# One series of scores for the first two token tiles of a differential head, a price for changes of rows in the planner, and the first norm's sums on VectorE

## The chip, the cores and the metric

The kernel runs on one core of a Trainium2 chip. The metric is the device time of one execution in microseconds (us), the median of several runs. Engines: PE is the matmul engine (PEld its weight loads), DVE is VectorE, ACT is ScalarE, POOL is GpSimd, SP issues the DMAs.

## The reference

A trunk of two residual layers on 512 tokens of 1024 features, in float32. Layer 0 mixes tokens with retention, layer 1 with differential attention in six heads; each layer also attends to 256 memory tokens and ends with a SwiGLU feed-forward part. What the change touches:

```python
def rms_norm(x, w):
    y = x32 * lax.rsqrt(jnp.mean(x32 * x32, axis=-1, keepdims=True) + EPS)
...
    h = rms_norm(x, attn_norm_w[layer])
    u = h @ w_in[layer]
...
        sc = jnp.einsum('bihcd,bjhcd->bhcij', qblk, k).astype(jnp.float32) * scale
        dist = jnp.abs(t[:, None] - s_pos[None, :]).astype(jnp.float32)
        bias = -slopes[:, None, None] * dist[None]
        allowed = s_chunk[None, :] <= (t // CHUNK)[:, None]
        sc = jnp.where(allowed, sc + bias[None, :, None], -jnp.inf)
        p = jax.nn.softmax(sc, axis=-1)
        a = p[:, :, 0] - lam * p[:, :, 1]
        return jnp.einsum('bhij,bjhe->bihe', a.astype(v.dtype), v)
```

A differential head has two score maps, each from 64 features, whose softmaxes are subtracted. Queries go in blocks of 128 tokens and see the keys up to their own chunk.

## The kernel before, in words

**Layout and precision.** x stands transposed in eight tiles `xT` of 128 features x 512 tokens. A float32 product is made of three matmuls of a faster type: each operand is split into a high half (`wh` of weights, made by ACT) and a low half (`wl`, the rest, made by DVE, or POOL in some chunks of layer 1), and `mm3` adds high by high, high by low and low by high. Weights come by DMA in chunks into three pages `wr`, and each chunk is split once, for three pages of either half.

**The planner.** The program is written out by Python, with one stream of main matmuls and many generators for side work (norms, softmaxes, transposes, splits). `Weave` keeps a clock for each engine. Each operation passes through `Engine.go` (lines 263 to 291), which counts a cost for it (`us`): a matmul of 128 rows with n columns n / 2400 + 0.0134; one with 64 rows 0.11 + 0.00012 n; a DVE operation 0.07 + 0.00104 n; a POOL addition 0.17 + 0.0021 n. It then moves that engine's clock, waiting for what the operands need. After each matmul of the main stream `pump` lets those side generators go on whose due time has come on PE's clock. So these costs set the order in which each engine's instructions stand; on the chip every engine takes them in that order. Pages and banks are counted in `free`; `take` waits until there are enough, `give` returns them.

**The first token norm.** For each feature tile `NormX.tile` (line 613) multiplies by the norm's weight, splits (ACT then DVE), waits (in the first norm alone 4.0 us, `later`), squares on ACT into a `tab` page of which there are three, and adds the square to the first tile's, on POOL (line 630). After the eighth, `token_norm` (line 544) sums over features with four small matmuls against ones, and the power -0.5 follows on POOL. Meanwhile the main stream runs the first projection (`tok_block`, `first=True`): chunk by chunk, 24 matmuls each, as tiles and chunks arrive. Splits of chunk 3 are queued on ACT and DVE when the stream comes to chunk 2.

**The differential heads.** `lane` (line 1248) starts the units of the two heads of a projected pair: for each head `unit` once for each of four token tiles a, as soon as the tile's queries and keys are ready and the unit before has sent its exponentials. `unit` (line 1132) makes the two score maps in two banks with `mm3_pair`: six matmuls of 64 rows and (a + 1) * 128 columns, in three pairs, the first map on partitions 0 to 63 and the second on 64 to 127. DVE adds the position bias and takes the minimum (the scores are negated); ACT exponentiates with the row sum; DVE forms the quotient `rho` and the difference of the maps. Every second unit transposes the differences of two tiles and multiplies by the values.

**The second norm's halves.** `token_halves` (line 1343) makes differences and sums of token halves for a fast matrix product, in `wk` pages.

Of the kernel before, what the change touches and what calls it, by code (L numbers as in the profile page):

```python
# [14 lines left out]
AF = mybir.ActivationFunctionType  # L15
# [3 lines left out]
P = 128  # L19
# [137 lines left out]
class Weave:  # L157
# [7 lines left out]
    def __init__(self):  # L165
        self.n, self.q = 0, []
        self.clock = {"pe": 0.0, "dve": 0.0, "act": 0.0, "pool": 0.0, "dma": 0.0}
        self.written = {}
        self.slots, self.slot, self.seen = {}, {}, {}
        self.port = {"dve": [], "pool": []}  # L170
        self.last = self.cur = self.now = 0.0
# [82 lines left out]
class Engine:  # L254
# [5 lines left out]
    def __getattr__(self, op):  # L260
        call = getattr(self.engine, op)

        def go(out, *args, **kw):
# [4 lines left out]
            if self.name == "pe":  # L268
                us = max(0.108, n / 2400 * (1 if op == "transpose" or kw["rhs"].dtype == F32R else 4) + 0.0134)
                if ins[0].shape[0] == 64:  # L270
                    us = 0.11 + 0.00012 * n
            elif self.name == "act":
                us = 0.09 + 0.00084 * n + 0.19 * ("accum_out" in kw) + 0.05 * isinstance(kw.get("scale"), bass.AP)
            elif self.name == "pool":
                us = 0.3 + 0.165 * n if kw.get("op") == ALU.pow else 0.17 + 0.0021 * n
            elif self.name == "dma":
                us = n * P * 4 / 360e3
            else:
                us = 0.07 + 0.00104 * n + 0.06 * any(free_size(v) == 1 and n > 1 for v in ins[1:])
# [13 lines left out]
def body(ctx: ExitStack, tc: tile.TileContext, x_d, mem_d, w_d, par_d, dec_d, ali_d, out_d):  # L293
# [309 lines left out]
    class NormX:  # L603
# [9 lines left out]
        def tile(self, k):  # L613
# [14 lines left out]
            else:  # L628
                yield
                G.tensor_tensor(self.sq_sum, self.sq_sum, sq, op=ALU.add)  # L630
# [453 lines left out]
    def diff_layer(layer, xw, nrm, mem_norm):  # L1084
# [47 lines left out]
        def unit(h, a, qT, kT, st):  # L1132
            n = (a + 1) * P
            u = a // 2
            ts = slice(a * P, (a + 1) * P)
            es = slice(h * P, (h + 1) * P)
            pages = st["pages"][u]
            if u == 0:
                pr = [pages[c][:, a * P:a * P + n] for c in range(2)]
            else:  # L1140
                pr = [pages[2 * (a - 2) + c][:, :n] for c in range(2)]
            st["p"][a] = pr[0]
            mn, s1, rho = small(2), small(2), small(1)
# [10 lines left out]
            for c in range(2):  # L1154

                V.tensor_tensor_reduce(pr[c], scs[c][:, :n], st["ali"][:, T - n:], scale=1.0, scalar=3.0e38,
                                       op0=ALU.add, op1=ALU.min, accum_out=mn[:, c:c + 1])
                ends.append(W.last + 0.13)
# [3 lines left out]
            for c in range(2):  # L1162
                W.cur = ends[c]
                yield
                dst = st["s0"][:, a:a + 1] if c == 0 else s1[:, 0:1]
                A.activation(pr[c], pr[c], AF.Exp, bias=mn[:, c:c + 1], scale=-1.0, accum_out=dst)
# [81 lines left out]
        def lane(p, res, ready):  # L1248
# [9 lines left out]
            for i in range(2):  # L1258
                st = {"ali": alis[i], "s0": page("s0", [P, TT], 6), "av": 0, "started": 0, "p": {}, "done": set(),
                      "pages": [[], []]}  # L1260
                for a in range(TT):
                    pages = 2 * (a // 2) + 2 if a % 2 == 0 else 0
                    while free["wk"] < pages or st["started"] < a or a not in ready or W.backlog() > BACKLOG:
                        yield 0.3
                    yield from take(wk=pages)
                    st["pages"][a // 2] += [wk([P, T]) for _ in range(pages)]
                    W.add(unit(2 * p + i, a, res[i], res[2 + i], st))
# [75 lines left out]
    def token_halves(layer, norm, tb):  # L1343
# [7 lines left out]
        def sums(j):  # L1351
# [5 lines left out]
            z = [wk([P, T])[:, s] for _ in range(3) for s in (a, b)]  # L1357
# [375 lines left out]
```

## Time and profile before

| what | us |
| --- | --- |
| median of 3 runs | 1141.38 |
| lowest and highest of them | 1139.38, 1141.46 |
| the profiled execution | 1143.51 |
| its span, first to last instruction | 1141.7 |
| mean granted clock of PE over the span | 0.997 of full |

Every instruction goes through line 287, so groups of the profile are told apart by engine, operation and tile names: `out<-in`, then the shape, then the count (x6). Two rows with one name in the timeline are merged where nothing else of that engine stands between. Times are from the span's start.

### The profile page before, as it was taken

What the parts mean: (1) busy time and instruction counts of PE and PEld (TensorE: products, weight loads), DVE (VectorE), ACT (ScalarE), POOL (GpSimd) and SP (SyncE); (2) the same over time, 40 slices, a digit from 0 to 9 for tenths busy, and PEclk for the clock granted to TensorE, in tenths of its full rate; (3) what the DMA queues carried; (4) which work ended last, traced back from release to release, by engine and by line L of the source; (5) the groups of instructions that cost most, each with busy time, mean ns of one, the idle gap of its engine ahead of it and who ended that gap; (6) DMA issues with size and microseconds to landing.
All of it is one profiled execution on the core that took longest, in us unless ns stands there. A gap on an engine that the chain in (4) does not pass through costs nothing.

```text
span 1141.7 us, 18447 instructions
## 1 busy us (share of the span) xinstructions
PE 1130.7 (99%) x6917; PEld 999.2 (88%) x6917; DVE 892.6 (78%) x1717; ACT 626.8 (55%) x1291; POOL 157.8 (14%) x105
## 2 busy tenths in 40 slices
PE   9999999999999999999999999999999999999998
PEld 7788888889999999998888877888899999999987
DVE  5669895799997878887657577967989987788862
ACT  6557773545564445555466575745556554455540
POOL 4120010400000000000362653343000000000000
PEclk9999999999999999999999999999999999999999
DMA  6341222332342333334231311122332333223332
GB/s 212 126 143 61 74 74 75 111 93 92 118 136 84 103 110 102 97 112 159 68 116 58 111 61 51 57 74 93 94 108 89 125 105 123 86 93 102 96 111 76
DMA packets 46600, 113.54 MB, mean 99 GB/s; under 512 B 5296, under 2 KB 17968, under 8 KB 46512
## 3 DMA queue, kind: packets, MB, share of 16 engines
q1 hardware_dynamic: 46368, 112.35, 30.5%
q8 instruction: 54, 0.88, 0.3%
q14 instruction: 34, 0.28, 0.1%
q10 hardware_dynamic: 144, 0.03, 0.0%
HBM read 110.26 MB, written 2.10 MB: 98 GB/s over the span
## 4 chain that ended last, share of the span: by engine, by line
PE 91%; DVE 3%; ACT 3%; POOL 1%; issue 1%; DMA 1%; SPq 0%; DVEq 0%; ACTq 0%
PE ps L287 91%; DVE wk L287 1%; POOL tab L287 1%; ACT wk L287 1%; DVE sm L287 1%; DMA wr<-w_t 1%; ACT wh L287 0%; DVE qk L287 0%; ACT qk L287 0%; ACT mkY L287 0%; DVE mkL L287 0%; SPq L287 0%; ACT L287 0%; ACT qc L287 0%; ACT xw L287 0%
## 5 line engine op out<-in xcount | busy, mean ns | idle before, releaser
L287 PE MATMUL ps<-xw,wh 128*128 128x256 f32 (+1 forms) x1032 | 211.6, 326 | 0.0
L287 ACT ACTIVATE wk<-ps 128x256 f32<-128x256 f32 (+3 forms) x214 | 90.8, 427 | 168.2 <-PE ps L287 167.2
L287 PE MATMUL ps<-xw,wl 128*128 128x256 f32 (+1 forms) x948 | 179.0, 306 | 0.0
L287 PEld LDWEIGHTS ps<-xw,wh 128*128 128x128 f32 x1032 | 154.4, 190 | 15.5
L287 PE MATMUL ps<-wh,xw 128*128 128x512 f32 (+1 forms) x512 | 151.1, 375 | 1.0 <-DVE qk L287 1.0
L287 PEld LDWEIGHTS ps<-xw,wl 128*128 128x128 f32 x948 | 131.2, 190 | 7.4
L287 PE MATMUL ps<-qk,wl 128*128 128x512 f32 (+1 forms) x528 | 135.6, 386 | 0.0
L287 ACT ACTIVATE wh<-wr 128x512 fp32r<-128x512 f32 (+1 forms) x144 | 118.6, 827 | 27.2 <-PE ps L287 20.9
L287 DVE TENSOR_TENSOR wl<-wk,wl 128x512 fp32r<-128x512 f32 (+3 forms) x150 | 94.4, 630 | 29.0 <-ACT wl L287 28.2
L287 PEld LDWEIGHTS ps<-qk,wl 128*128 128x128 f32 x528 | 96.1, 188 | 18.3
L287 ACT ACTIVATE wl<-wk 128x512 fp32r<-128x512 f32 (+3 forms) x150 | 85.6, 571 | 40.1 <-DVE wk L287 25.7
L287 PEld LDWEIGHTS ps<-wh,xw 128*128 128x128 f32 x512 | 92.8, 191 | 16.5 <-DVE qk L287 1.5
L287 POOL TENSOR_TENSOR tab<-tab,tab 128x512 f32<-128x512 f32 x31 | 47.2, 1524 | 431.9 <-DVE v L287 306.7
L287 PE MATMUL ps<-v,wh 128*128 128x256 f32 x792 | 106.1, 279 | 0.0
L287 PE MATMUL ps<-qk,wh 128*128 128x512 f32 (+1 forms) x393 | 104.4, 387 | 0.5 <-DVE qk L287 0.5
L287 DVE TENSOR_TENSOR wh<-wk,wh 128x512 fp32r<-128x512 f32 (+3 forms) x130 | 79.2, 609 | 26.7 <-ACT wh L287 26.7
L287 PEld LDWEIGHTS ps<-v,wh 128*128 128x128 f32 x792 | 98.3, 189 | 0.0
L287 PE MATMUL ps<-wl,xw 128*128 128x512 f32 (+1 forms) x256 | 96.0, 375 | 0.9 <-DVE wl L287 0.9
L287 ACT ACTIVATE wh<-wk 128x512 fp32r<-128x512 f32 (+3 forms) x130 | 72.6, 559 | 42.5 <-DVE wk L287 34.6
L287 DVE TENSOR_TENSOR xT<-ps,xT 128x512 f32<-128x512 f32 (+1 forms) x81 | 55.1, 680 | 50.9 <-PE ps L287 50.6
L287 PEld LDWEIGHTS ps<-qk,wh 128*128 128x128 f32 x393 | 71.9, 188 | 15.6 <-DVE qk L287 1.1
L287 PE MATMUL ps<-v,wl 128*128 128x256 f32 x576 | 77.4, 279 | 0.0
(169 smaller groups left out, 1969.7 us busy)
## 6 DMA issues: line engine op xcount, KB each, us to landing
wr<-w_t SPq DMA_DIRECT2D x148, 512.0 KB, 3.5
wk<-w_t SPq DMA_DIRECT2D x48, 192.0 KB, 3.8
wk<-w_t SPq DMA_DIRECT2D x32, 256.0 KB, 3.9
wk<-w_t SPq DMA_DIRECT2D x32, 128.0 KB, 3.4
wr<-w_t SPq DMA_DIRECT2D x8, 256.0 KB, 5.2
xT<-x_t SPq DMA_DIRECT2D x8, 256.0 KB, 5.5
zo<-mem_t SPq DMA_DIRECT2D x8, 256.0 KB, 6.0
out_t<-xT SPq DMA_DIRECT2D x7, 256.0 KB, 2.0
```

The source lines that it names most:

```text
L287: return call(out, *args, **kw)
```

## The change

Four things. (1) `Engine.go` adds 0.19 to a matmul whose rows differ from those of the matmul before it. (2) The sums of the squares of the norm with `later` (the first) go to DVE. (3) `unit` takes a group of token tiles: (0, 1) in one unit, then 2, then 3. The group's scores lie side by side in the same two banks and are made in one run of twelve matmuls; the minimum passes, exponentials, one reciprocal and one `rho` for the group follow. A group starts when its last tile is ready. (4) `token_halves` takes three `wk` pages and cuts each in two halves, where it called for six pages.

```diff
+        self.rows = 128
...
                 if ins[0].shape[0] == 64:
                     us = 0.11 + 0.00012 * n
+
+                us += 0.19 * (ins[0].shape[0] != self.weave.rows)
+                self.weave.rows = ins[0].shape[0]
...
-                G.tensor_tensor(self.sq_sum, self.sq_sum, sq, op=ALU.add)
+                (V if self.later else G).tensor_tensor(self.sq_sum, self.sq_sum, sq, op=ALU.add)
...
-        def unit(h, a, qT, kT, st):
-            n = (a + 1) * P
+        def unit(h, group, qT, kT, st):
+            a, g = group[-1], len(group)
...
+            cols = {b: slice(b * P, b * P + (b + 1) * P) if u == 0 else slice(0, (b + 1) * P) for b in group}
+            pr = {b: [pages[c if u == 0 else 2 * (b - 2) + c][:, cols[b]] for c in range(2)] for b in group}
+            mn, s1, rho = small(2 * g), small(2 * g), small(g)
             yield from take(ps=2)
-            scs, pair = [bank(), bank()], []
-            for c in range(2):
-                rows = slice(c * DH, (c + 1) * DH)
-                pair.append((scs[c][:, :n], [z[rows, ts] for z in qT], [z[rows, :n] for z in kT]))
-            mm3_pair(pair)
+            scs = [bank(), bank()]
+            for b in group:
+                st["p"][b] = pr[b][0]
+                ts, keys, pair = slice(b * P, (b + 1) * P), slice(0, (b + 1) * P), []
+                for c in range(2):
+                    rows = slice(c * DH, (c + 1) * DH)
+                    pair.append((scs[c][:, cols[b]], [z[rows, ts] for z in qT], [z[rows, keys] for z in kT]))
+                mm3_pair(pair)
...
-            V.reciprocal(s1[:, 1:2], s1[:, 0:1])
-            V.scalar_tensor_tensor(rho, st["s0"][:, a:a + 1], lam, s1[:, 1:2], op0=ALU.mult, op1=ALU.mult)
+            V.reciprocal(s1[:, g:2 * g], s1[:, :g])
+            V.scalar_tensor_tensor(rho, st["s0"][:, group[0]:a + 1], lam, s1[:, g:2 * g], op0=ALU.mult, op1=ALU.mult)
 
-            V.scalar_tensor_tensor(pr[0], pr[1], rho, pr[0], op0=ALU.mult, op1=ALU.add)
-            st["done"].add(a)
+            for i, b in enumerate(group):
+                V.scalar_tensor_tensor(pr[b][0], pr[b][1], rho[:, i:i + 1], pr[b][0], op0=ALU.mult, op1=ALU.add)
+            st["done"].update(group)
...
-                for a in range(TT):
-                    pages = 2 * (a // 2) + 2 if a % 2 == 0 else 0
-                    while free["wk"] < pages or st["started"] < a or a not in ready or W.backlog() > BACKLOG:
+                for group in ((0, 1), (2,), (3,)):
+                    a = group[-1]
+                    pages = (2, 4, 0)[a - 1]
+                    while free["wk"] < pages or st["started"] < group[0] or a not in ready or W.backlog() > BACKLOG:
...
-            z = [wk([P, T])[:, s] for _ in range(3) for s in (a, b)]
+            z = [w[:, s] for w in [wk([P, T]) for _ in range(3)] for s in (a, b)]
```

## Rows read from the trace of the kernel before

**Rows 1.** The page, part 1: busy us (share of the span) and instructions by engine.

```profile
PE 1130.7 (99%) x6917; PEld 999.2 (88%) x6917; DVE 892.6 (78%) x1717; ACT 626.8 (55%) x1291; POOL 157.8 (14%) x105
```

**Rows 2.** Windows: stretch, us, busy of PE, PEld, DVE, ACT, POOL, PE's clock, DMA, GB/s.

```profile
650.00:675.00 25.00, 24.65 (x143) 18.26 (x142) 16.38 (x62) 14.13 (x39) 9.71 (x6) 1.00 0.30 97
675.00:700.00 25.00, 23.78 (x140) 18.55 (x139) 20.14 (x60) 16.57 (x47) 11.16 (x8) 1.00 0.21 69
800.00:825.00 25.00, 25.00 (x115) 20.77 (x114) 24.71 (x56) 14.59 (x28) 1.02 (x1) 1.00 0.33 98
```

**Rows 3.** Timeline of PE, 23 to 34: start, us, what, [idle before <-releaser].

```profile
23.21 0.74 PE L287 MATMUL ps<-wh,xw 128*128 128x512 f32 x2
24.52 0.50 PE L287 MATMUL ps<-wl,xw 128*128 128x512 f32 x1 [0.57 <-DVE wl L287]
25.66 1.52 PE L287 MATMUL ps<-ones,tab 128*128 128x1 f32 x8 [0.63 <-POOL tab L287]
27.03 1.20 PE L287 MATMUL ps<-wh,xw 128*128 128x512 f32 x2
28.03 0.63 PE L287 MATMUL ps<-wl,xw 128*128 128x512 f32 x1
28.46 1.05 PE L287 MATMUL ps<-wh,xw 128*128 128x512 f32 x2
...
33.04 0.39 PE L287 MATMUL ps<-wl,xw 128*128 128x512 f32 x1
```

**Rows 4.** A window of 1 us there: columns as in rows 2.

```profile
31.00:32.00 1.00, 1.00 (x4) 0.79 (x3) 0.75 (x2) 0.24 (x2) 0.68 (x1) 0.50 0.70 244
```

**Rows 5.** Timelines of POOL, ACT and DVE, 14 to 28.

```profile
14.88 10.72 POOL L287 TENSOR_TENSOR tab<-tab,tab 128x512 f32<-128x512 f32 x7 [13.57 <-ACT tab L287]
...
20.88 0.63 ACT L287 ACTIVATE tab<-xT 128x512 f32<-128x512 f32 x1 [0.74 <-POOL tab L287]
...
22.79 2.51 ACT L287 ACTIVATE wh<-wr 128x512 fp32r<-128x512 f32 x3
...
14.50 0.75 DVE L287 SCALAR_TENSOR_TENSOR xw<-xT,par,xw 128x512 fp32r<-128x512 f32 x1
15.96 0.99 DVE L287 SCALAR_TENSOR_TENSOR xw<-xT,par,xw 128x512 fp32r<-128x512 f32 x1 [0.72 <-ACT xw L287]
22.07 0.70 DVE L287 TENSOR_TENSOR wl<-wr,wh 128x512 fp32r<-128x512 f32 x1 [5.11 <-ACT wh L287]
23.43 4.38 DVE L287 TENSOR_TENSOR wl<-wr,wh 128x512 fp32r<-128x512 f32 x3 [0.67 <-ACT wh L287]
```

**Rows 6.** Timeline of PE around two series of 64 rows, 652 to 657.

```profile
652.91 0.62 PE L287 MATMUL ps<-wh,xw 128*128 128x512 f32 x2
653.47 0.55 PE L287 MATMUL ps<-qk,qk 64*128 64x128 f32 x6
653.95 0.50 PE L287 MATMUL ps<-wl,xw 128*128 128x512 f32 x1
654.28 0.63 PE L287 MATMUL ps<-wh,xw 128*128 128x512 f32 x2
654.75 0.40 PE L287 MATMUL ps<-wl,xw 128*128 128x512 f32 x1
655.07 0.62 PE L287 MATMUL ps<-qk,qk 64*128 64x256 f32 x6
655.62 0.74 PE L287 MATMUL ps<-wh,xw 128*128 128x512 f32 x2
656.21 0.40 PE L287 MATMUL ps<-wl,xw 128*128 128x512 f32 x1
```

**Rows 7.** Timelines of PE and DVE: a wait, and two small operations of a unit.

```profile
685.00 0.50 PE L287 MATMUL ps<-wh,xw 128*128 128x512 f32 x1 [1.02 <-DVE qk L287]
...
673.16 0.15 DVE L287 RECIPROCAL sm<-sm 128x1 f32<-128x1 f32 x1
673.35 0.22 DVE L287 SCALAR_TENSOR_TENSOR sm<-s,der,sm 128x1 f32<-128x1 f32 x1
```

More of the change, by code (lines that the diff above doesn't have):

```diff
@@ L1130, in qk_proj @@
             W.add(lane(p, res, ready))
-        def unit(h, a, qT, kT, st):
-            n = (a + 1) * P
+        def unit(h, group, qT, kT, st):
+            a, g = group[-1], len(group)
             u = a // 2
-            ts = slice(a * P, (a + 1) * P)
             es = slice(h * P, (h + 1) * P)
             pages = st["pages"][u]
[L1138 to L1143, printed above, removed]
-            yield from take(ps=2)
-            scs, pair = [bank(), bank()], []
-            for c in range(2):
-                rows = slice(c * DH, (c + 1) * DH)
-                pair.append((scs[c][:, :n], [z[rows, ts] for z in qT], [z[rows, :n] for z in kT]))
-            mm3_pair(pair)
+            cols = {b: slice(b * P, b * P + (b + 1) * P) if u == 0 else slice(0, (b + 1) * P) for b in group}
+            pr = {b: [pages[c if u == 0 else 2 * (b - 2) + c][:, cols[b]] for c in range(2)] for b in group}
+            mn, s1, rho = small(2 * g), small(2 * g), small(g)
+            yield from take(ps=2)
+            scs = [bank(), bank()]
[6 more added lines that the diff above has]
+                mm3_pair(pair)
             if a == TT - 1:
@@ L1153, in unit @@
             ends = []
[L1154 to L1158, printed above, removed]
+            for i, b in enumerate(group):
+                for c in range(2):
+                    V.tensor_tensor_reduce(pr[b][c], scs[c][:, cols[b]], st["ali"][:, T - (b + 1) * P:], scale=1.0, scalar=3.0e38,
+                                           op0=ALU.add, op1=ALU.min, accum_out=mn[:, 2 * i + c:2 * i + c + 1])
+                    ends.append(W.last + 0.13)
             give("ps", 2)
@@ L1161, in unit @@
                 give("tab", 1)
[L1162 to L1166, printed above, removed]
+            for i, b in enumerate(group):
+                for c in range(2):
+                    W.cur = ends[2 * i + c]
+                    yield
+                    dst = st["s0"][:, b:b + 1] if c == 0 else s1[:, i:i + 1]
+                    A.activation(pr[b][c], pr[b][c], AF.Exp, bias=mn[:, 2 * i + c:2 * i + c + 1], scale=-1.0, accum_out=dst)
             st["started"] = a + 1
             yield
-            V.reciprocal(s1[:, 1:2], s1[:, 0:1])
-            V.scalar_tensor_tensor(rho, st["s0"][:, a:a + 1], lam, s1[:, 1:2], op0=ALU.mult, op1=ALU.mult)
-            V.scalar_tensor_tensor(pr[0], pr[1], rho, pr[0], op0=ALU.mult, op1=ALU.add)
-            st["done"].add(a)
+            V.reciprocal(s1[:, g:2 * g], s1[:, :g])
+            V.scalar_tensor_tensor(rho, st["s0"][:, group[0]:a + 1], lam, s1[:, g:2 * g], op0=ALU.mult, op1=ALU.mult)
+            for i, b in enumerate(group):
+                V.scalar_tensor_tensor(pr[b][0], pr[b][1], rho[:, i:i + 1], pr[b][0], op0=ALU.mult, op1=ALU.add)
+            st["done"].update(group)
             if a % 2 == 0:
@@ L1266, in lane @@
                     st["pages"][a // 2] += [wk([P, T]) for _ in range(pages)]
-                    W.add(unit(2 * p + i, a, res[i], res[2 + i], st))
+                    W.add(unit(2 * p + i, group, res[i], res[2 + i], st))
                     yield 0.5
```

## The prediction

> **What bounds the kernel now.** I read the page first, then the windows of 25 us, then PE's timeline where a window looked odd. The page has PE busy for 99% of the span [rows 1], so a saving counts only if it takes work or waiting off PE itself, and a cost only if PE waits for it. That busy share hides something: PE's record of a matmul runs on while it waits inside the pipeline, and what tells of lost time is the weight loads, of which each matmul has one. In an ordinary stretch, 800 to 825, they are busy for 20.8 of 25 us; in 650 to 675, with PE still at 24.65, only for 18.3 [rows 2]. From there on I measure lost time by the starts of successive matmuls. A full 128x512 matmul takes 0.23 us from start to start (two from 654.28 to 654.75 [rows 6]). Two places of the change lose time by that measure.
>
> *The start.* From 23.21 to 33.04 us PE needs 9.83 us for 17 matmuls of 512 columns (2, 1, 2 and 12 in rows that alternate) and the eight small ones of the first token norm [rows 3]. At full pace these are 17 x 0.23 = 3.9, and about 0.9 for the eight (they took 1.37, most of it at half clock, so between 0.7 and 1.4). So 5.0 us are lost: first a wait for a weight split (0.57 idle, DVE wl), then one for the last sum (0.63 idle, POOL tab), and behind the two the granted clock falls to 0.5, from 2.4 to 1.2 GHz, until about 33 us: 128x512 matmuls have a spacing of 0.43 (28.03 to 28.46), and the window at 31 shows the clock [rows 3, 4]. Both waits go back to POOL. Its seven sums run from 14.88 for 10.72 us, 1.53 each. ACT's squares wait for the pages that they free (0.74 idle before the one at 20.88), the weight split's ACT half stands behind those squares and starts at 22.79, and DVE, after 5.11 us without work, gets its half late and then takes 4.38 us for three splits, of which the first kind alone takes 0.70: it runs slowly beside POOL [rows 5].
>
> *The score series.* A series of six 64-row matmuls costs PE, for 128 columns, 654.28 - 652.91 = 1.37 less three ordinary ones, 0.68 us; for 256 columns 656.21 - 654.75 = 1.46 less three, 0.77 us [rows 6]. The six run as three pairs side by side. Three pairs at half of 0.23 would be 0.35 for 256 columns, which leaves 0.42; for 128 columns the pairs can't cost more than that, which leaves at least 0.33. So 0.33 to 0.42 of each series is a fixed price of entering and leaving it, seen as late starts on both sides: 653.47 where the row before would end its turn at 653.37, and 0.33 instead of 0.23 behind 653.95.
>
> **The change, part by part.** The sum is made against the profiled execution, 1143.51 us (span 1141.7 and 1.8 around it), which lies 2.1 over the median of 1141.38; differences are carried to the median.
>
> *Sums on VectorE.* Seven POOL additions go, seven DVE additions come, at 0.65 to 0.70 each by the 128x512 TENSOR_TENSOR at 22.07 [rows 5]: 4.9 us of DVE work into a stretch where it idles 5.11 and 0.72. Squares still need the three tab pages, each freed by the sum before last. DVE is done with the seventh tile's split at 14.50 + 0.75 = 15.25. From there seven sums and the last token tile's split (0.75) run back to back to 20.9, or to 21.6 if the first weight split of chunk 3 gets in ahead of the last sum. The order of PE is set by the planner: with 0.60 in place of 1.245 for a sum, and the last square still held 4 us behind its split, I count the norm's matmuls some 15 places into chunk 2, whose first matmul stands at 17.3 (chunk 3's is two matmuls ahead of the row at 23.21, at 22.8, and 24 at the planner's 0.227 come before it). PE comes there at 17.3 + 15 x 0.227 = 20.7. An estimate from both: a wait of 0.2 to 0.9, and I take 0.9. Queued on DVE behind sums that wait for squares are the splits of chunk 3, which PE wants at 22.8 and which, sent straight after, are ready by about 22: no second wait. One pause of 0.9 is shorter than the two together, and around the idle 1.02 at 685.00 [rows 7] the granted clock stayed at 1.00 [rows 2], so I take it to stay up. Gain 5.0 - 0.9 = 4.1; between 0 (the pause and the fall stay) and 5.0 (no pause).
>
> *One series for token tiles 0 and 1.* Six heads lose one entry and exit each. No row has a series that changes its width inside. The bounds are 0 (the width costs what the row change costs) and 0.42; the nearest row is the series itself, whose pairs change their weights twice without a late start of that size, so I take 0.36: 6 x 0.36 = 2.2 us.
> The Trainium skill (TensorEngine Tiling (Array Packing), section Key Properties) says that changing the tiling mode, not just the tile, drains the engine. By that a change of width inside the series drains nothing and the 2.2 stand, where the lower bound above would make them 0; no run here has shown such a series yet.
>
> *DVE beside it.* One reciprocal (0.15) and one small product (0.22) [rows 7] go per head, 2.2 us in all, under PE's matmuls and worth nothing where they are covered. At 685.00, where PE idles 1.02 for DVE, they may take up to 0.4 off; I count 0.2. The four minimum passes now stand in one block on DVE and hold two banks until the last of them, 0.4 to 0.8 us longer; what waits behind it is the next projection's norm, and that is how the wait at 685.00 came about, so this may also give those 0.2 back. The first pair of scores also waits for the second token tile, 6 x 0.23 = 1.4 us later; the lane has the next projection's matmuls as cover, and without it PE would wait those 1.4 once.
>
> *The estimate.* Before, the planner took 6 x (0.11 + 0.00012 x 128) = 0.75 for a series that measures 0.68, and 0.84 for 0.77: right within 0.07. It now adds 0.19 for each change of rows to a price that already held it. A series at 384 or 512 columns is over by 0.38; the joined one is put at 0.75 + 0.84 + 0.38 = 1.97 against 0.68 + 0.77 - 0.36 = 1.09, over by 0.88. Over six heads that is 6 x (0.88 + 0.38 + 0.38) = 9.8 us by which PE arrives before the planner expects it, at transposes and products whose input another engine is still making. Cover: the exit's part is right for work that starts from that series (its end and the next matmul's delay are now put where the trace has them), and waits that the planner itself foresees on PE are swallowed first. I take a sixth, 1.6 us of new waits, between 0 and 9.8.
>
> *Page reuse in the second norm's halves.* Three wk pages per pair in place of six names for them; the instructions are the same. At 800 to 825, with DVE at 24.7 of 25, PE was full [rows 2]: nothing. If that cover went, a late split of 0.7 per pair would show.
>
> Sum: -4.1 - 2.2 - 0.2 + 0.2 + 1.6 = -4.7: 1138.8 for this execution, 1136.7 against the median.
>
> **The rivals.**
> - *The pause keeps its price* (chance 0.12). The sums on DVE still end after PE arrives, PE pauses as long as before and the clock falls. For it: the planner moves PE's place forward by nearly as much as the sum. Against it: 5.11 us of DVE idle and no POOL beside it. The start then gains nothing: 1136.7 + 4.1 = 1140.8, no change to be told.
> - *The padded estimate becomes waits* (0.08). At the transposes and value products of layer 1, 650 to 760 us, PE stands for what it is ahead of the plan. All 9.8 in place of 1.6 give 1136.7 + 8.2 = 1144.9, slower. It decides from 6.3 us of new waits on (4.7 + 1.6). Against it: only one wait of that stretch exceeds 0.5 now, so the side work is not always late to the last moment.
> - *The join saves nothing* (0.07): the change does on PE what it did before, 1136.7 + 2.2 = 1138.9, still faster by 0.2%.
> - *All of it helps* (0.10): no pause at the start, the wait at 685.00 gone (1.0) and no new ones: 1136.7 - 0.9 - 1.0 - 1.6 = 1133.2.
>
> **How the numbers follow.** My forecast has 0.63 (1134.5 to 1138.9, by a pause from 0 to 1.5 and new waits from 0.5 to 3). A measurement of this kernel tells about 0.2% from no change: under 1139.1 is faster, over 1143.7 slower. Faster: 0.63 + 0.10 + 0.07 = 0.80. Same: 0.12 and half of the padded estimate, 0.16. Slower: 0.04. The range from 1133.2 to 1140.6 leaves out most of the second rival and the tails of the first and last, under 2 in 10.
>
> **What would show it.** Right: in the profile after, POOL has nothing before the norm's power; the eight small matmuls stand near 21 us with a wait of under 1 us, the granted clock stays at 1.0 through 25 to 33; there are 18 series of 64 rows, six of them with twelve matmuls that cost about 1.1 us; weight loads in 650 to 675 gain. Wrong: a clock of 0.5 before 35 us; a late start inside the joined series; several waits of PE for ACT or DVE over 0.5 us between 650 and 760 us, with a sum above 3.

## The result and the profile after

The changed kernel takes 1149.46 us (median of 5 runs, 1148.53 to 1150.43), the kernel before 1139.58 beside it (1139.38 to 1141.46): a ratio of 1.0084 [1.0072, 1.0095]. It is slower by 9.9 us. The forecast was 1136.7, 0.80 for faster and 0.04 for slower. It was wrong, and two things went wrong apart from each other: a gain that was counted does not exist in most executions, and a cost that was counted at 1.6 us is several times that.

The profiled execution took 1148.70 us. Part 1 of its page, answering [rows 1], and its windows, answering [rows 2] and with the same columns:

```profile
PE 1128.9 (98%) x6917; PEld 996.1 (87%) x6917; DVE 895.1 (78%) x1712; ACT 626.8 (55%) x1291; POOL 147.6 (13%) x98
```

```profile
650.00:675.00 25.00, 23.94 (x139) 17.14 (x135) 17.52 (x59) 13.94 (x40) 5.80 (x3) 1.00 0.17 52
675.00:700.00 25.00, 22.31 (x141) 17.12 (x141) 22.93 (x66) 17.50 (x51) 12.52 (x7) 1.00 0.21 74
800.00:825.00 25.00, 25.00 (x116) 20.73 (x115) 24.55 (x51) 15.89 (x31) 3.72 (x3) 1.00 0.30 92
```

PE is busy for 1.8 us less and the span is 5.2 longer, so PE waits more. The windows say where: weight loads fall from 18.26 to 17.14 and from 18.55 to 17.12 in the two stretches of layer 1's attention, while 800 to 825 stands as before. What PE waits for there, by the view of waits on PE over 640 to 775 us (for what, then us in total, times, longest), before and after:

```profile
PE ps L287 <- DVE qk L287: 1.0, 1, 1.0
PE ps L287 <- ACT wk L287: 0.6, 3, 0.2
PE ps L287 <- DVE wk L287: 0.2, 1, 0.2
```

```profile
PE ps L291 <- DVE wk L291: 4.0, 5, 1.8
PE ps L291 <- DVE zo L291: 2.9, 4, 2.0
PE ps L291 <- DVE qk L291: 1.4, 1, 1.4
PE ps L291 <- DVE sm L291: 0.2, 1, 0.2
PE ps L291 <- ACT qk L291: 0.2, 1, 0.2
```

1.8 us of visible idle became 8.7, and DVE ends nearly all of it: the transposes of a head's differences (wk), of its output (zo), the projections' evacuation (qk). Six of the waits between 650 and 760 us are over 0.5, 5.5 us together: the sign of being wrong that the prediction named.

Since a PE record runs on while its matmul waits in the pipeline, I use a second measure for all kernels below and call it **the stage's waits**: over 640 to 775 us, the distance from each matmul's end to the next one's, less what its width takes in an unbroken row (0.227 us for 512 columns, 0.118 for 256, 0.109 for 128), summed, less the time of the 64-row series themselves (20.6 us for 24 series, 18.6 for 18), with what stretches at half clock cost counted apart. It gives 3.9 before and 15.3 after. The sum closes. An execution of a kernel whose start and stage are those of before (the kernel with only the page reuse, 1139.58 us, span 1137.8) has 4.0 us of such waits and no half clock: 15.3 - 4.0 of new waits, less 2.0 for the joined series, are 9.3, and the spans differ by 1146.9 - 1137.8 = 9.1.

The timeline of PE at the start and at a joined series, answering [rows 3] and [rows 6], and the window of [rows 4]:

```profile
19.82 0.39 PE L291 MATMUL ps<-wh,xw 128*128 128x512 f32 x1
20.82 1.05 PE L291 MATMUL ps<-ones,tab 128*128 128x1 f32 x8 [0.61 <-DVE tab L291]
21.74 0.49 PE L291 MATMUL ps<-wh,xw 128*128 128x512 f32 x1
...
657.93 0.39 PE L291 MATMUL ps<-wl,xw 128*128 128x512 f32 x1
658.25 0.96 PE L291 MATMUL ps<-qk,qk 64*128 64x128 f32 x12
659.14 0.73 PE L291 MATMUL ps<-wh,xw 128*128 128x512 f32 x2
659.71 0.39 PE L291 MATMUL ps<-wl,xw 128*128 128x512 f32 x1
```

```profile
31.00:32.00 1.00, 1.00 (x7) 0.87 (x6) 1.00 (x3) 0.70 (x3) 0.94 (x2) 1.00 0.97 377
```

The norm's small matmuls stand at 20.82 behind one wait of 0.61, and the granted clock stays at 1.00: as forecast for this execution. The joined series costs 659.71 - 657.93 = 1.78 less three ordinary matmuls, 1.09 us: as forecast to the hundredth (0.68 + 0.77 - 0.36).

### The profile page after: what moved, and what is told of

It is laid out like the page before. It is cut to its first block, busy times and chain, and to the rows that moved or that the text cites. A ratio compares the mean times of both kernels' runs of the same rounds, so it can differ in the third digit from the quotient of the medians.

```text
span 1146.9 us, 18449 instructions
## 1 busy us (share of the span) xinstructions
PE 1128.9 (98%) x6917; PEld 996.1 (87%) x6917; DVE 895.1 (78%) x1712; ACT 626.8 (55%) x1291; POOL 147.6 (13%) x98
## 4 chain that ended last, share of the span: by engine, by line
PE 86%; DVE 4%; ACT 4%; issue 3%; DMA 1%; POOL 1%; SPq 0%; ACTq 0%; POOLq 0%; DVEq 0%
PE ps L291 86%; DVE wk L291 2%; ACT wk L291 2%; DMA wr<-w_t 1%; DVE sm L291 1%; ACT wh L291 1%; ACT qk L291 1%; DVE qk L291 0%; POOL wl L291 0%; POOL sm L291 0%; ACT mkY L291 0%; DVE mkL L291 0%; SPq L291 0%; ACT tab L291 0%; ACT qc L291 0%
## 5 line engine op out<-in xcount | busy, mean ns | idle before, releaser
L291 PE MATMUL ps<-wh,xw 128*128 128x512 f32 (+1 forms) x512 | 148.3, 370 | 0.6 <-DVE wk L291 0.6
L291 POOL TENSOR_TENSOR tab<-tab,tab 128x512 f32<-128x512 f32 x24 | 37.0, 1541 | 423.0 <-DVE v L291 306.7
L291 PEld LDWEIGHTS ps<-qk,wh 128*128 128x128 f32 x393 | 71.8, 188 | 15.3 <-DVE qk L291 1.1
```

Source lines behind the costliest of these rows:

```text
L291: return call(out, *args, **kw)
```

## The experiments

Four theories stood after this. **T1**: the padded price makes the planner believe that PE comes later than it does, so side work is placed too late. **T2**: the joined unit itself costs (four minimum passes and four exponentials in one block, a later start). **T3**: any new order of this finely balanced stage loses. **T4**: DVE's operations in the units' chains (scores, minimum, exponential, difference, transpose) stand still while POOL makes its weight splits. All results in one table; "over" is by how much the planner's price for the stage's series exceeds what they take (the price called right below lies 0.8 under it, and stands as 0, with the versions made from it counted from there), and "waits" is the stage's waits, with what half clock costs behind a plus.

| kernel | units, splits of layer 1, over (us) | median us | ratio to before | waits |
| --- | --- | --- | --- | --- |
| before | separate, POOL, 0.8 | 1139.5 | 1 | 3.9 |
| changed | joined, POOL, 9.8 | 1149.46 | 1.0084 [1.0072, 1.0095] | 15.3 |
| e1_sums_only | separate, POOL, 0.8 | 1139.65 | 1.0002 [0.9992, 1.0011] | 3.9 |
| e2_pages_only | separate, POOL, 0.8 | 1139.64 | 1.0003 [0.9994, 1.0013] | 4.0 |
| e1_price_only | separate, POOL, 9.9 | 1146.96 | 1.0069 [1.0051, 1.0087] | 11.0 + 1.4 |
| e2_before_right | separate, POOL, 0 | 1139.82 | 1.0002 [0.9993, 1.0012] | 4.0 |
| e2_join_only | joined, POOL, 3.0 | 1145.09 | 1.0050 [1.0035, 1.0065] | 9.8 + 2.3 |
| e1_no_price | joined, POOL, 3.0 | 1144.61 | 1.0036 [1.0022, 1.0051] | 9.7 + 1.6 |
| e1_right_price | joined, POOL, 0 | 1142.19 | 1.0022 [1.0013, 1.0032] | 6.7 + 2.2 |
| e2_right_half | joined, POOL in halves, 0 | 1145.28 | 1.0051 [1.0035, 1.0068] | 9.8 + 1.5 |
| e2_after_half | joined, POOL in halves, 9.8 | 1145.36 | 1.0051 [1.0036, 1.0066] | 11.0 |
| e2_right_dve | joined, DVE, 0 | **1136.98** | 0.9982 [0.9972, 0.9991] | 3.0 |
| e3_after_dve | joined, DVE, 9.8 | 1145.52 | 1.0056 [1.0041, 1.0071] | 11.0 |
| e3_before_dve | separate, DVE, 0.8 | 1146.60 | 1.0067 [1.0052, 1.0082] | 8.2 + 2.1 |
| e4_over_half | joined, DVE, 4.9 | 1139.89 | 1.0006 [0.9996, 1.0016] | 5.6 |
| e4_under | joined, DVE, -6.5 | 1137.01 | 0.9978 [0.9969, 0.9988] | 2.7 |
| e4_right_in_pool | joined, POOL for input projections, 0 | 1143.08 | 1.0033 [1.0021, 1.0045] | 7.9 + 1.9 |
| e5_right_act | as e1_right_price, no POOL splits | 1138.06 | 0.9984 [0.9975, 0.9994] | 4.5 |
| e5_after_act | as the changed kernel, no POOL splits | 1148.75 | 1.0078 [1.0061, 1.0095] | 14.4 + 1.3 |
| e5_before_act | as before, no POOL splits | 1142.88 | 1.0032 [1.0021, 1.0044] | 7.3 |

### The parts alone

e1_sums_only is the kernel before with one line of the change:

```diff
-                G.tensor_tensor(self.sq_sum, self.sq_sum, sq, op=ALU.add)
+                (V if self.later else G).tensor_tensor(self.sq_sum, self.sq_sum, sq, op=ALU.add)
```

> The kernel before with nothing but the first norm's sums on DVE. All theories: one wait of 0.5 to 0.9 us at the eight small matmuls near 21 us, the granted clock at 1.0 from 25 to 33 us, the order of layer 1 as before. The profiled execution of before lost 5.0 us there, which would give 1135.5. The five timed executions of before (1139.4 to 1141.5) lie 2 to 4 us under that profiled one, so part of those 5.0 may be the fall of the clock in that one execution alone; then the gain is 1 to 2.5 and the time 1137 to 1138.5.

It changes nothing, where 1137 to 1138.5 was expected: 1139.65, with an interval of 0.1% to either side of 1. The 4.1 us of the forecast are not there, and e2_pages_only shows why. It has the page line alone:

```diff
-            z = [wk([P, T])[:, s] for _ in range(3) for s in (a, b)]
+            z = [w[:, s] for w in [wk([P, T]) for _ in range(3)] for s in (a, b)]
```

> The kernel before with nothing but three pages in place of six in the second norm's halves. All theories: 1139 to 1140.5, no wait of PE in 200 to 250 or 800 to 850 us that the kernel before has not.

Every engine's order is that of before. In its profiled execution, the timeline of PE and the window of 1 us:

```profile
23.71 0.50 PE L287 MATMUL ps<-wl,xw 128*128 128x512 f32 x1
24.84 1.05 PE L287 MATMUL ps<-ones,tab 128*128 128x1 f32 x8 [0.63 <-POOL tab L287]
25.75 0.70 PE L287 MATMUL ps<-wh,xw 128*128 128x512 f32 x2
26.30 0.39 PE L287 MATMUL ps<-wl,xw 128*128 128x512 f32 x1
26.52 0.62 PE L287 MATMUL ps<-wh,xw 128*128 128x512 f32 x2
```

```profile
31.00:32.00 1.00, 1.00 (x7) 0.77 (x6) 0.77 (x2) 0.96 (x4) 0.00 (x0) 1.00 0.97 344
```

The wait for the last sum is the 0.63 of [rows 3], the one for the split nearly gone, and behind them matmuls run 0.22 to 0.23 apart (26.30, 26.52): the clock of 0.50 of [rows 4] did not come. It belongs to some executions. Of 88 runs of the kernel before that stand beside these experiments, seven take 1141.3 to 1141.9, with a mean clock of 0.998 or 0.999 over the span; the other 81 take 1138.9 to 1140.2, and the 71 runs at 1.000 have a median of 1139.5. The profiled execution with its 0.997 and 1143.51 was of the longer kind, as were, by their times, two of the three runs behind the median of 1141.38. Nor does the moved sum abolish the fall: in the profile of e1_sums_only the clock reads 0.50 from 22.6 to 26.0, behind one wait of 1.08 for the last sum:

```profile
24.00:25.00 1.00, 1.00 (x4) 0.81 (x3) 0.04 (x1) 0.00 (x0) 0.00 (x0) 0.50 0.71 279
```

The page reuse costs nothing, as forecast. The price alone, on the kernel before (e1_price_only):

```diff
+        self.rows = 128
...
+                us += 0.19 * (ins[0].shape[0] != self.weave.rows)
+                self.weave.rows = ins[0].shape[0]
```

> The kernel before with nothing but the added 0.19 for a change of rows. 24 series are then priced 0.38 over what they take, 9.1 us together. Theory 1: PE is ahead of the side work in 650 to 770 us by up to that, waits of 5 to 9 us come up there, and the time is 1144 to 1149. Theory 2: the units are as before, so 1139 to 1141. Theory 3: 1141 to 1146, with the waits in other places than the changed kernel's.

It loses 7.4 us with not one instruction added or taken away, and its waits rise by 7. The two converses, the changed kernel without those lines (e1_no_price) and the kernel before with the joined unit alone (e2_join_only):

> The changed kernel with the added 0.19 for a change of rows taken out of the estimate; the joined series, the sums on DVE and the page reuse stay. If the padded estimate is what costs (theory 1), the new waits of 650 to 770 us mostly go: PE's weight loads there come back, the joined series still cost 1.09 us each, and the time is 1134 to 1138, under the kernel before. If the joined unit itself is what costs (theory 2: four minimum passes and four exponentials in one block, a start that waits for the second token tile), the waits stay: 1146 to 1150. If any new order of that stage loses against the old one, whatever is estimated (theory 3), something between, 1141 to 1146.

> The kernel before with the joined unit alone: no price for a change of rows, sums on POOL, six pages in the halves. The old price puts a joined series at 0.75 + 0.84 = 1.59 where 1.09 is measured, 0.50 too high, 3.0 us over six heads, a third of the padded price's 9.8. The run with sums and page reuse besides gave 1144.6 (waits 9.7). If the join with that price is the cause there: 1143 to 1146 and waits of 8 to 11. If sums or page reuse had a part in it: under 1141.

They agree with each other (9.7 and 9.8 us of waits), and both are slower than before. The first lies where T3 had it (1141 to 1146), not where T1 did (1134 to 1138). So the joined unit loses about 5 us by itself where the price is left as it was, and the price lines another 5 on top of it. But "as it was" is not right for a joined unit: the old formula gives its twelve matmuls 0.75 + 0.84 = 1.59 for a series that takes 1.09, over by 0.5, 3.0 us for six heads. T1 and T2 had to be parted by a price that is right for either form.

### The right price

Half of a 128-row matmul's price for one of 64 rows, which run in pairs, and 0.18 for each change of rows:

```diff
                 if ins[0].shape[0] == 64:
-                    us = 0.11 + 0.00012 * n
+                    us = max(0.108, n / 2400 + 0.0134) / 2
-                us += 0.19 * (ins[0].shape[0] != self.weave.rows)
+                us += 0.18 * (ins[0].shape[0] != self.weave.rows)
```

It gives 1.04 for the joined series, which takes 1.09, and 0.68 and 0.72 for the two separate ones, which take 0.68 and 0.77. On the changed kernel, and on the kernel before as a control:

> The changed kernel with the price of 64-row matmuls set to what the trace has: half of a 128-row matmul each (they run in pairs) and 0.18 for each change of rows, so 0.68 for a series of 128 columns where 0.68 is measured, and 1.04 for the joined one where 1.09 is measured. Theory 1: no systematic lead of PE, waits in 650 to 770 us no larger than in the kernel before, 1133 to 1136, the fastest of the four. Theory 2: 1146 to 1150 as the changed kernel. Theory 3: anywhere from 1136 to 1146.

> The kernel before, units one by one, with nothing but the price of 64-row matmuls set to the trace: half of a 128-row matmul each and 0.18 for a change of rows, 0.68 for a series of 128 columns that the kernel before puts at 0.75. A control for theory 1: the price moves by 0.07 a series at most, 1.0 us over 24, downwards. If only a price that is too high costs, nothing happens: 1139 to 1141, waits of PE in 640 to 775 us about 4 as in the kernel before. If any reordering of that stage costs (theory 3), 1141 to 1145, with waits of 6 or more.

On separate units the right price costs and gains nothing, though it moves the order as much as the padded one: by the traces, 202 of DVE's 1717 instructions stand in another place than before, and 184 in e1_price_only, which loses 7.4. On the joined ones it takes 7.3 us off the changed kernel, so T1 holds for the larger part of the loss, but not for all of it: T1 alone asked for 1133 to 1136. What is left, 2.7 us above before, lies in few places. The timelines of DVE, POOL and PE there, in e1_right_price:

```profile
736.52 0.22 DVE L291 SCALAR_TENSOR_TENSOR sm<-s,der,sm 128x2 f32<-128x2 f32 x1
736.77 5.04 DVE L291 SCALAR_TENSOR_TENSOR wk<-wk,sm,wk 128x128 f32<-128x128 f32 x2
...
736.82 2.37 POOL L291 TENSOR_TENSOR wl<-wr,wh 128x1024 fp32r<-128x1024 f32 x1 [10.45 <-ACT wh L291]
739.14 2.39 POOL L291 TENSOR_TENSOR qc<-wr,qc 128x1024 fp32r<-128x1024 f32 x1
...
739.39 0.33 PE L291 MATMUL ps<-ident,wk 128*128 128x128 f32 x1 [1.57 <-DVE wk L291]
741.88 0.69 PE L291 MATMUL ps<-ident,wk 128*128 128x128 f32 x2 [2.16 <-DVE wk L291]
```

The two differences of a joined unit take 5.04 us. In e2_right_dve the same two take 0.75 (a row of it stands below). Each takes 2.56, and they end 0.15 and 0.28 us behind the ends of POOL's two splits, and PE, at the transposes, waits 1.57 and 2.16 for them. From 739.8, behind the first of these waits, the clock is granted at half for 6.8 us, which costs the 2.2 in the table's last column:

```profile
742.00:746.00 4.00, 4.00 (x11) 3.23 (x12) 3.93 (x11) 1.90 (x5) 2.05 (x1) 0.50 0.63 168
```

By the Trainium skill (SBUF — State Buffer, section Who interferes with whom) a VectorE instruction with two inputs in SBUF contends with a GpSimd instruction that reads SBUF, and the one issued first has the shared port for the whole of its instruction while the other is fully blocked. The trace agrees in kind: 5.04 us in place of 0.75, ending with POOL's instructions. Which was issued first it doesn't tell, as the two records start 0.05 us apart. The same happens in the changed kernel, where the held operation is a tiny one that stands ahead of the minimum passes; its timelines of POOL, DVE and PE:

```profile
670.57 2.40 POOL L291 TENSOR_TENSOR wl<-wr,wh 128x1024 fp32r<-128x1024 f32 x1 [11.21 <-ACT wh L291]
...
670.79 2.19 DVE L291 SCALAR_TENSOR_TENSOR sm<-sm,sm 128x4 f32<-128x4 f32 x1
672.91 0.68 DVE L291 CUSTOM_DVE_ANT_0 wk<-ps,tab 128x512 f32<-128x512 f32 x1
...
676.11 0.75 DVE L291 SCALAR_TENSOR_TENSOR wk<-wk,sm,wk 128x512 f32<-128x512 f32 x1
...
676.92 0.88 PE L291 MATMUL ps<-ident,wk 128*128 128x128 f32 x6 [1.82 <-DVE wk L291]
```

2.19 us for 128x4, up to the end of POOL's 2.40, then minimum, exponential, difference, and PE waits 1.82.

Before, DVE is held as well, and the wait of [rows 7] has such an operation in its chain. DVE and POOL there:

```profile
682.47 1.03 DVE L287 SCALAR_TENSOR_TENSOR sm<-s,der,sm 128x1 f32<-128x1 f32 x1
684.21 0.74 DVE L287 SCALAR_TENSOR_TENSOR qk<-ps,der,qk 128x512 fp32r<-128x512 f32 x1
...
681.07 2.42 POOL L287 TENSOR_TENSOR wl<-wr,wh 128x1024 fp32r<-128x1024 f32 x1
```

The small product takes 1.03 in place of the 0.22 of [rows 7], and two operations later comes the evacuation that PE waits for at 685.00. What DVE's operations of the stage take beyond the shortest of their form, counted from 0.25 us on, is 5.5 us before, 6.5 in the changed kernel and 5.6 in e1_right_price. So the change hardly made DVE stand still for longer; it moved which operations do, and where these lie in a chain that PE waits for, they cost. The planner counts such holds too (`port` in `Weave.run`), but by its own clocks; why these came in front of PE all the same, no run shows.

### POOL's splits

Two ways out of that: shorter instructions on POOL, or none. e2_right_half and e2_after_half cut them in halves; e2_right_dve gives them to DVE, in both cases with the planner knowing of it.

```diff
+                for part in (slice(0, wL.shape[1] // 2), slice(wL.shape[1] // 2, wL.shape[1])):
+                    G.tensor_tensor(wL[:, part], raw[:, s][:, part], f(wH)[:, part], op=ALU.subtract)
-                G.tensor_tensor(wL, raw[:, s], f(wH), op=ALU.subtract)
```

```diff
-                G.tensor_tensor(wL, raw[:, s], f(wH), op=ALU.subtract)
+                split_l(wH, wL, raw[:, s])
```

> The changed kernel with the right price and with each of POOL's weight splits of layer 1 (2.4 us, in which a DVE operation on two SBUF tiles was seen to take 2.56 in place of 0.35) cut into two of half the columns. Theory 4: what is left against the price is DVE held up by those long POOL splits; halved, the 2.5 us wait of PE at 742 and the fall of the clock behind it go, waits of 640 to 775 us come to 4 or less, and the time is 1135 to 1138, under the kernel before. Theory 3: a new order again, 1140 to 1145, with waits elsewhere.

> The changed kernel as it is, its padded price too, with POOL's weight splits of layer 1 cut in halves. Theory 1: the price keeps PE ahead of the side work, waits of 640 to 775 us stay over 10 (15 in the changed kernel), the time is 1145 to 1149. Theory 4: most of the 15 us come from DVE held up by POOL; waits fall to 4 to 8, the time to 1139 to 1143.

> The changed kernel with the right price and POOL's weight splits of layer 1 given to DVE (12 operations of about 1.2 us in 640 to 775 us, where DVE is busy for 96 of 132 us). Theory 4: no DVE operation takes longer than its like any more, and the waits of PE that came from that go, but DVE has 14 us more to do; 1136 to 1141. Theory 2 or 3: waits of 6 or more stay in the stage, 1141 to 1146.

Halves don't help the right-priced kernel (3.1 us worse, where T4 asked for less than before), and take 4.1 us off the changed one, with 11.0 of waits left as T1 had it: a miss for any single rule. The halves run back to back, so a chain of several DVE operations is held once for each. In e2_right_half, DVE and PE (the operations' usual 0.22 and 0.6 us become 1.18 and 1.59):

```profile
742.57 1.18 DVE L291 SCALAR_TENSOR_TENSOR sm<-s,der,sm 128x1 f32<-128x1 f32 x1
743.78 1.59 DVE L291 SCALAR_TENSOR_TENSOR wk<-wk,sm,wk 128x384 f32<-128x384 f32 x1
...
746.28 1.01 PE L291 MATMUL ps<-wk,v 128*128 128x128 f32 x6 [3.57 <-DVE v L291]
```

Giving the splits to DVE does help: 1136.98 us, 0.18% under before and 12.5 under the changed kernel, the first version to gain. Its waits on PE in the stage are one row, and the two differences of the joined unit stand between DVE's own splits at full pace:

```profile
PE ps L291 <- DVE qk L291: 0.3, 1, 0.3
```

```profile
739.47 1.22 DVE L291 TENSOR_TENSOR wl<-wr,wh 128x1024 fp32r<-128x1024 f32 x1
...
741.05 0.75 DVE L291 SCALAR_TENSOR_TENSOR wk<-wk,sm,wk 128x128 f32<-128x128 f32 x2
741.72 1.22 DVE L291 TENSOR_TENSOR wl<-wr,wh 128x1024 fp32r<-128x1024 f32 x1
```

The controls are the same line on the changed kernel (e3_after_dve) and on the kernel before (e3_before_dve):

> The changed kernel, its padded price as it is, with POOL's weight splits of layer 1 given to DVE: no DVE operation of the stage can be held up by POOL any more, so what waits of PE remain come from the order alone. Against the run with the right price and the same splits on DVE (1137.0, waits of 3.0 us in 640 to 775 us) it differs in the price only. Theory 1 (the price makes PE arrive early, POOL or no POOL): waits of 7 to 12, 1141 to 1147. Theory 4 (the padded price costs only because it moves DVE's operations under POOL's splits): waits of 3 to 5, 1137 to 1139.

> The kernel before with POOL's weight splits of layer 1 given to DVE: a control for the version that beats both. If the gain of that version is the splits' alone, this one gains as much: 1136 to 1138. If it is the join (18 series in place of 24, 2.2 us, and 0.4 us of small DVE operations a head less) that pays once the order fits, this one does not gain: 1139 to 1144, with DVE busier than in the kernel before.

On the changed kernel it takes off 3.9 us and leaves 11.0 of waits, so the padded price does harm without POOL's splits. On the kernel before it costs 7.1, so the splits on DVE don't gain by themselves; separate units with the right price and the splits on DVE were not run. And with only the output projection's splits on DVE:

```diff
-            if key[1] == 1 and (key[0] == "in" or key[0] == "out" and key[2] <= NOUT):
+            if key[1] == 1 and key[0] == "in":
```

> e2_right_dve with the weight splits of the second layer's input projections left on POOL, and only those of its output projection on VectorE. T4 (VectorE's operations in the chains of the joined units stand still behind POOL's 2.4 us splits, and it is those that lie under a chain that cost): if the splits of the output projection are the ones that do it, waits of 3 to 4 us and 1136 to 1138 us; if those of the input projections do, waits of 5.5 to 7.5 us and 1140 to 1142.5 us, as e1_right_price with all of them on POOL (6.7 us, 1142.2 us). Rival T5 (not the standing still but VectorE's place in the written order): waits that follow neither, above 8 us, with VectorE's operations at their usual lengths.

In the main wait POOL has no part: it has no instruction from 733 to 741. DVE and PE there:

```profile
737.36 1.22 DVE L291 TENSOR_TENSOR qc<-wr,qc 128x1024 fp32r<-128x1024 f32 x1
738.49 1.22 DVE L291 TENSOR_TENSOR wl<-wr,wh 128x1024 fp32r<-128x1024 f32 x1
739.63 0.55 DVE L291 TENSOR_TENSOR wk<-ps,wk 128x384 fp32r<-128x384 f32 x1
740.10 0.74 DVE L291 SCALAR_TENSOR_TENSOR qk<-ps,der,qk 128x512 fp32r<-128x512 f32 x1
...
740.89 0.79 PE L291 MATMUL ps<-qk,wh 128*128 128x512 f32 x1 [4.38 <-DVE qk L291]
```

PE waits 4.38 us for an evacuation that stands behind two splits, each at its usual length, and before them behind the four minimum passes of a joined unit (1.2 us). That is the rival T5 in kind, at 7.9 us where it asked for over 8. These runs all moved the order along with the splits, so three more keep the written order: the planner counts POOL's splits as before, but a copy by ACT stands in their place.

```diff
-                G.tensor_tensor(wL, raw[:, s], f(wH), op=ALU.subtract)
+                G.tensor_tensor(wL, raw[:, s], f(wH), act=nc.scalar, op=ALU.subtract)
...
+            if act:
+                return act.activation(out, args[0], AF.Copy)
```

> e1_right_price (joined, right price, splits on POOL; 1142.2 us, stage waits 6.7) with its written order unchanged: the planner goes on counting each of POOL's 26 weight splits of the second layer as POOL's, but the instruction at that place is a copy by ScalarE of the same 128x1024, right behind ScalarE's own split of the upper part. Left out of the computation: the lower part of those weights (the copy writes the whole weight there). POOL is then idle where its 2.4 us operations were, VectorE's own list is the same. T4 (the operations that VectorE holds until POOL's end make TensorE wait): waits fall to 2.5 to 4.5 us and the time to 1137 to 1140. Rival T5 (the written order makes them; the long VectorE operations lie in slack): waits stay at 6 us or more, 1141.5 us or more. ScalarE's 1 us more per split in the chains speaks against T4 only.

> The same edit on the changed kernel (1149.5 us, stage waits 15.3 in its profile), written order unchanged; the lower part of the same weights is left out. T4: waits fall by 3 to 5 us, to 10 to 12 (what e3_after_dve had with another order), 1144.5 to 1146.5 us. Rival T5: waits of 14 us or more, 1148.5 us or more.

> The same edit on the kernel before (1139.5 us, stage waits 3.9), written order unchanged; the lower part of the same weights is left out. T4 as far as it goes: before has its held VectorE operations too, in front of slack in most places, so waits of 2.5 to 4 us and 1138 to 1139.6 us. If it gains as much as the joined kernels (waits under 1 us, 1136 us or less), the hold is no part of what the change lost. Rival T5: no change, 3.9 us and 1139.5.

With the right price T4 holds: the same order without POOL's splits is 4.1 us faster (2.2 of waits and 2.2 of half clock), though ACT has more to do. PE's waits for wk in the stage, in e1_right_price and in e5_right_act, and the two differences that took 5.04 us, in e5_right_act:

```profile
PE ps L291 <- DVE wk L291: 3.7, 2, 2.2
```

```profile
PE ps L293 <- DVE wk L293: 0.6, 2, 0.3
```

```profile
737.74 0.75 DVE L293 SCALAR_TENSOR_TENSOR wk<-wk,sm,wk 128x128 f32<-128x128 f32 x2
```

On the changed kernel it gains 0.7 only, where T4 asked for 3, and both numbers lie where T5 had them: the 1.82 at 676.92 is gone, others came. The control says that these copies have a price of their own, which neither theory had: before gets 3.4 us slower. Its largest row of waits on PE in the stage is ACT's:

```profile
PE ps L289 <- ACT wk L289: 2.4, 4, 1.8
```

So in the changed kernel POOL's share of the loss is not settled: 0.7 us with the order kept and ACT burdened, 3.9 with another order (e3_after_dve).

### How a price becomes waits

On the version with the splits on DVE, where POOL makes none of these splits, the price per change of rows is 0, 0.18, 0.315 or the padded one:

```diff
-                us += 0.18 * (ins[0].shape[0] != self.weave.rows)
+                us += 0.315 * (ins[0].shape[0] != self.weave.rows)
```

> e2_right_dve with 0.315 us per change of rows in place of 0.18. The stage's 36 changes are then put at 4.9 us more than they cost, half of what the padded price of the changed kernel puts on them; joined unit and VectorE splits unchanged. T1 (what is put on top comes back as waits of TensorE, about us for us, whatever share it is): waits in the stage (640 to 775 us) of 6 to 9 us where e2_right_dve had 3.0 and e3_after_dve 11.0, and 1139 to 1142.5 us. Rival T1b (a fixed harm, one reordering of the stage that any wrong price sets off): waits near 11 and 1144.5 to 1146.5. Rival T1c (some over-price is slack that the late side work uses up first): waits under 4.5 and 1136 to 1138.

e4_under has 0.0 there.

> e2_right_dve with nothing per change of rows: the 36 changes are put at 6.5 us less than they cost. T1 one-sided (only a price that is too high makes TensorE come ahead of its side work; one that is too low makes side work early, which costs nothing): stage waits of 2 to 4 us and 1136 to 1138 us, as e2_right_dve. Rival T1d (an order written by any wrong price is worse, either way): waits of 7 us or more and 1140 us or more.

Over by -6.5, 0, 4.9 and 9.8 us, the stage waits 2.7, 3.0, 5.6 and 11.0 us, and the kernel takes 1137.01, 1136.98, 1139.89 and 1145.52. Too low a price costs nothing here; the first half of what is put on top costs 2.9 us of time (0.6 of it), the second 5.6 (all of it and a little more). The 5.6 us of waits lie just under the 6 to 9 that T1 gave, and far from a fixed harm of 11. On separate units with POOL's splits, 9.1 us put on top cost 7.4. T3, as a rule for any new order, falls by e2_before_right and e4_under, which lose nothing; that some orders do lose at a price that is right, or 0.8 over, e4_right_in_pool and e3_before_dve show. T2, as a cost of the joined unit by itself, falls by e2_right_dve, which has that unit.

## Why the prediction was wrong

**Sums on VectorE: wrong.** The forecast took 4.1 us from a stretch of one profiled execution. What it said of that stretch came true (20.82, one wait of 0.61, full clock), but 3.1 of its 5.0 us were the half clock, which most executions of the kernel before never had, and most of the wait for the split was missing in e2_pages_only too. The step that failed was to carry a difference worked out on an execution of 1143.51 to the median; three runs of which two lay at 1141.4 and one at 1139.4 showed two levels, and the lower was the usual one. That the clock stayed up here was in part luck: of thirteen profiled executions with the sums on DVE it fell in four. Without the fall, the two starts lose about the same: 4.6 us over the first 45 us in e2_pages_only, 4.4 in the changed kernel.

**One series: right.** 1.09 us for twelve matmuls, 18 series; 2.0 us off PE, where 2.2 stood. The Trainium skill (TensorEngine Tiling (Array Packing), section Key Properties) says that a change of the tiling mode, and not just of the tile, drains the engine. The trace agrees: inside the joined series at 658.25 the first pair of 256 columns starts 0.11 us behind the last pair of 128, as the pairs of 128 do among themselves.

**DVE beside it: right at 685 by luck, silent on what mattered.** The wait of [rows 7] is gone, but the prediction put it down to banks held by the minimum passes, and the held product in its chain (1.03 us at 682.47) was overlooked: in e5_before_act, with the same order and no POOL splits, 0.50 of its 1.02 us are left. The part named the block of minimum passes, but neither that part nor any other asked what a chain of the joined unit loses if one of its operations falls under a POOL split, though [rows 5] had shown DVE slow beside POOL at the start. With the right price this is worth 4.1 us (e5_right_act); with the padded one it is not settled.

**The estimate: the term that was mis-sized.** "I take a sixth, 1.6 us", of 9.8. The over-price itself was worked out rightly to about 0.2 (with 18.6 us for the stage's series it is 9.6), the twelve matmuls' 0.88 per head included. Its conversion into waits was a guess with no row behind it, and that is the step that failed. Measured: 7.4 of 9.1 on the kernel before, and 8.5 of 9.8 with the splits on DVE (1145.52 - 1136.98). The cover named for it, waits that the planner itself foresees, can have taken up no more than part of the first half, of which 0.6 came back; no run measures it alone. The argument against the rival, that only one wait exceeded 0.5 before, was read the wrong way round. Few waits in a stage written by a nearly right price don't mean that there is room: 4.9 us put on top of the right price already cost 2.9 in e4_over_half.

**Page reuse: right.** Nothing.

The rival "the padded estimate becomes waits" came true in its place, between 650 and 765 us, and in its sign (chance 0.08). It stood 3.5 us over the median it was made against; the 9.9 measured are that, the 4.1 that the start didn't give, 1.5 of waits beyond the whole over-price (11.3 for 9.8), 0.2 of the join (2.0 for 2.2), and 0.6 that the profiled execution doesn't show: it took 1148.70 at a mean clock of 1.000, while three of the five runs have 0.997 to 0.999 and take 1149.5 to 1150.4. The 9.1 us between the profiled executions of the changed kernel and of e2_pages_only are 11.3 of new waits less 2.0 for the join, to 0.2. Of the new waits the over-price accounts for most: 15.3 falls to 6.7 (and 2.2 of half clock) with the right price alone, and to 3.0 with POOL's splits moved too.

## What to carry to other kernels

Where a planner's costs write the order of the instructions, price a stretch by what it takes, entry and exit included, and compare a new term with the trace before it is added on top of one that already holds it; put too high, it came back here at 0.6 to 1.1 us for each us as waits of the engine that it was meant to describe; put too low, it cost nothing in the one case tried. Before counting a stall that a profile shows, ask whether every execution has it: the spread of the run times and the mean clocks beside them tell. A GpSimd instruction of 2.4 us held a VectorE one of 0.16 for 2.19, so look which chain stands under it.

## What the runs showed that was not expected

The clock's fall at the start comes in one execution of an order and stays away in the next, and the waits in front of it differ as well. In the seven profiled executions with the sums on POOL the wait for the last sum is 0.63 or 0.64 us. The wait for the split ahead of it is 0.56 or 0.57 in three (before, e1_price_only, e2_before_right), and the clock falls from 2.4 to 1.2 GHz in these; it is 0.27 or nothing in four, and the clock stays. With the sums on DVE there is one wait: 0.96 to 1.75 in four executions with a fall, 0.86 or less in eight without, and 1.40 in one without (e2_after_half). So the longer waits and the fall go together in all but one; why the waits differ was not looked into. Seven of 88 runs of before take some 2 us more, at a mean clock of 0.998 or 0.999, and three of ten of e4_over_half take 2 to 4 us more, at 0.997 to 0.999 (1141.9 to 1144.0 beside 1139.4 to 1140.3).

Moving work off POOL, which is busy 13% of the time, is worth 4 to 5 us with the right price, and halving its instructions there costs 3; in the trace the halves stand back to back. What a change of the written order is worth depends on the price beside it: the same splits on DVE cost 7.1 us on the kernel before, and gain 3.9 on the changed one and 5.2 on the right-priced one.

The version that beats both kernels is e2_right_dve: the joined unit, the right price, the weight splits of layer 1 on VectorE (e4_under, with no price for a change of rows, is as fast). It gains 0.18%, 2.5 us; the joined series take 2.0 less, and the rest is a wait or two.
